# Down products of a two-chunk SwiGLU stage by seven block products, with one chunk's residual kept in DRAM

## The chip, the cores and the metric

One core of a Trainium2 chip runs the whole program. The metric is the device time of one execution in microseconds (us); the profile is one further execution, taken by the hardware profiler. TensorE appears as PE (its weight loads as PEld), VectorE as DVE, ScalarE as ACT, GpSimd as POOL and SyncE as SP. A transfer issued from SP and one issued from POOL go through different queues to the same 16 DMA engines.

## What is computed

A trunk of two layers over 1024 tokens of width 1024. Each layer has a token mixer and a SwiGLU network of inner width 2816, both behind an RMS norm with a learned shift and scale, both added to the residual x with a gate:

```python
for i in range(DEPTH):
    ...
    x = x + (1.0 + g_m)[:, None, :] * y
    h = modulate(rms_norm(x, norm_ffn_g[i]), sh_f, sc_f)
    y = swiglu_ffn(h, ffn_w_gate[i], ffn_w_up[i], ffn_w_down[i])
    x = x + (1.0 + g_f)[:, None, :] * y
return rms_norm(x, final_g)

def swiglu_ffn(h, w_gate, w_up, w_down):
    return (jax.nn.silu(h @ w_gate) * (h @ w_up)) @ w_down
```

The change concerns the last product, `@ w_down`, in a part of layer 1.

## The kernel before

**Layout.** Channels lie on the 128 partitions, tokens along a row. The tokens are cut into two chunks of 512, A and B. x is held as 8 tiles of 128x512 per chunk; the inner width is 22 tiles f of 128 channels.

**Precision.** A float32 operand is split into a rounded part (hi, a cast on ACT) and the rest (lo, a subtraction on DVE, or on early weights a negated copy on ACT and an accumulating transfer from POOL). A product of two such operands is three matmuls: hi by hi, hi by lo, lo by hi.

**The two-chunk part.** In layer 1 the tiles f = 8 to 21 are taken in 7 pairs for both chunks at once (`ffn_joint`). A pair has a gate unit and an up unit (`joint_unit`). In a unit the 2x2 block product (two halves of the width by two chunks, against two f tiles) is done with seven block products in place of eight, the scheme of Strassen and Winograd: blocks w11, w12, s2, s1, s3, s4 and w22, each of 4 steps of 3 matmuls, 84 in all. The sums s1 to s4 of the weights are made on DVE; the sums t1 to t4 of the activations are too large to be all in SBUF, so t1 and t4 lie in DRAM and are read into the same 8 buffers by turns in each unit (`streamed`, issued from SP).

**The down products** of a pair run inside the two units of the next pair, between those steps: after the steps counted in `GATE_SLOTS` and `UP_SLOTS` a unit calls `JointDowns.slot`, which makes one 128x512 output tile for one chunk: 2 f tiles by 3 matmuls into one of two spare PSUM banks, then `update` (a SCALAR_TENSOR_TENSOR on DVE: x = bank times gate plus x). Each unit has 8 such slots, 4 output tiles by two chunks; a pair has 16, or 96 matmuls. The downs of the last pair have no unit around them: `alone` runs them in two runs of 48 matmuls, between the first pieces of the chunk-B part that follows. The first pair of units instead carries the downs of chunk A for f = 6 and 7.

**Order.** The PE order is the order of the program text. The other engines are ordered by a scheduler with priorities; within an engine everything runs in that order, so an instruction that waits holds all behind it. Two PSUM pools matter here: `bank` (6 buffers, used in turn) and `spare_bank` (2 buffers).

**After the two-chunk part** chunk B does f = 0 to 7 alone (`ffn_mixed`), and `final(A)`, the last norm of chunk A, runs beside it.

Of the kernel before, what the change touches and what calls it, by code (L numbers as in the profile page):

```python
# [16 lines left out]
P = 128  # L17
# [55 lines left out]
for _name, _w in (  # L73
    ("ada_b", DEPTH * 6 * KT), ("norm_mix_g", DEPTH * KT), ("norm_ffn_g", DEPTH * KT),
    ("conv_b1", 2 * KT), ("conv_bdw", KT), ("conv_ln_g", KT), ("conv_ln_b", KT), ("conv_b2", KT),
    ("c", KT), ("pool_ls", KT), ("final_g", KT), ("conv_wdw", CW * KT),
):
    _COLS[_name] = _n
    _n += _w
NVEC = _n  # L80

# [41 lines left out]
def trunk(ctx, tc, xT, c, vec, ada, adan, w1, w2, wgu, wdn, wpl, wph, out):  # L123
# [43 lines left out]
    cst = ctx.enter_context(tc.tile_pool(name="cst", bufs=1))  # L167
    slots = ctx.enter_context(tc.tile_pool(name="slots", bufs=2 * KT))
# [132 lines left out]
    x = [[cst.tile([P, ch.n], F32, name=f"x_{ch.i}_{k}") for k in range(KT)] for ch in chunks]  # L301
# [9 lines left out]
    recip = cst.tile([P, PHALO], F32, name="recip")  # L311
# [4 lines left out]
    ccols = cst.tile([P, KT, 32], F32, name="ccols")  # L316
# [13 lines left out]
    uhalo = cst.tile([P, KT, HALO], F32, name="uhalo")  # L330
# [385 lines left out]
    class Taps:  # L716
# [10 lines left out]
        def step(self, e):  # L727
# [3 lines left out]
            w = lambda j: V("conv_wdw", j * KT + p)  # L731
# [47 lines left out]
    class Phased:  # L779
# [36 lines left out]
        def back(self):  # L816
            b = bank("pz")
            cols = b.rearrange("p (s q) -> p q s", q=PH)
            for q in range(PH):
                for g in range(PH):  # L820
                    matmul(cols[32 * g : 32 * g + 32, q, :], ident[:, 32 * q : 32 * q + 32], self.y[:, g * P : g * P + P], start=True, stop=True)
            clock["PE"] -= 2.5
            p = self.p
            u = st["u", 0, p]
            w = lambda j: V("conv_wdw", j * KT + p)
# [515 lines left out]
    def alone(downs, later=None):  # L1341

        def emit(take):
            if later is not None:
                later.fetch()
            while downs.todo:
                downs.slot(lambda n: output(n, True))
                if later is not None and len(downs.todo) == 4:
                    later.load(later.dps[0])
            reserve[0] = 0  # L1350
        return emit, ()
# [80 lines left out]
    class JointDowns(Downs):  # L1432


        def __init__(self, l, fs, dps, chs):
            super().__init__(None, l, fs, dps)
            self.todo = [(d, ch) for d in self.todo for ch in chs]

        def slot(self, out=None):
            d, ch = self.todo.pop(0)  # L1440
# [3 lines left out]
            for i, f in enumerate(self.fs):  # L1444
                g = st["g", ch.i, f]
                for j, (wp, a) in enumerate(((0, 0), (0, 1), (1, 0))):
                    matmul(b, wt[:, wp, i, (d % 2) * P : (d % 2 + 1) * P], g[a], start=i + j == 0, stop=i == 1 and j == 2)
            update(ch, d, b, gate_f, self.l)
            if d % 2 == 0:
                self.load(d // 2 + 1)  # L1450
            pace()
# [67 lines left out]
    def joint_unit(l, me, following, downs, later, first=False, last=False):  # L1519

        def emit(take):
# [8 lines left out]
            name = ("gate", "up")[me.which]  # L1530
            a, left, right = bank(name), bank(name), bank(name)
# [3 lines left out]
            slots_at = () if first else (GATE_SLOTS, UP_SLOTS)[me.which]  # L1535
            at = [0]

            def block(out, part, acts, start):
                for k, act in enumerate(acts):
# [5 lines left out]
                    if at[0] in slots_at and downs:  # L1545
                        for each in downs:
                            if each.todo:
                                each.slot()
                                break
            block(a, "w11", ha[:half], True)  # L1550
            S_.copy(ra, a)
            block(left, "w12", ha[half:], True)
            V_.tensor_tensor(ra, ra, left, op=ADD)
            if last:
# [5 lines left out]
            if first:  # L1560
                for each in downs:
                    while each.todo:
                        each.slot(lambda n: output(n, True))
                finish(T["rows"])
# [9 lines left out]
            else:  # L1574
                used[0] -= 2
# [3 lines left out]
            if later is not None:  # L1579
                later.load(later.dps[0])  # L1580
            block(right, "s4", hb[half:], False)
            V_.tensor_tensor(rb, rb, right, op=ADD)
            if last:
# [9 lines left out]
            if me.which == 0:  # L1593
# [3 lines left out]
            else:  # L1597
                sg = st["sg"]
                qa = temp(512)
                V_.tensor_tensor(ra, ra, sg[0], op=MUL)  # L1600
                V_.scalar_tensor_tensor(qa, a, -1.0, sg[3], op0=MUL, op1=MUL)
                V_.tensor_tensor(rb, rb, sg[1], op=MUL)
                V_.scalar_tensor_tensor(qb, qb, -1.0, sg[2], op0=MUL, op1=MUL)
                if len(st["G"]) == 2:
                    st["G"] += [raws.tile([P, D], F32R, tag="raw", name=nm("gpair")), wide("gpair", F32R)]
                for t, home, (ch, f) in zip((ra, qa, rb, qb), st["G"], ((A, 0), (A, 1), (B, 0), (B, 1))):
                    hi, lo = home[:, FRONT], home[:, BACK]
                    S_.copy(hi, t)
                    V_.tensor_tensor(lo, t, f32(hi), op=SUB)
                    st["g", ch.i, me.f + f] = hi, lo  # L1610
# [3 lines left out]
    def ffn_joint(l, start):  # L1614

        mates = [Joint(l, f, which) for f in range(start, NF, 2) for which in range(2)]
        mine = [[JointDowns(l, (start - 2, start - 1), dps, (A,)) for dps in ((0, 1), (2, 3))], []]
        for f in range(start, NF, 2):
            mine += [[JointDowns(l, (f, f + 1), dps, (A, B))] for dps in ((0, 1), (2, 3))]
# [110 lines left out]
    load_next(vecs, vec)  # L1730
    S_.activation(ccols[:, :, 0], V("c", 0, KT), AF.Silu)
    scale_b = cst.tile([P, KT], F32, name="scale_b")
# [311 lines left out]
    add(last[:1] + before[1:] + last[1:])  # L2044
# [56 lines left out]
```

## Time and profile before

| | before |
|---|---|
| median of 3 runs | 1777.24 us (1776.34 to 1777.5) |
| the profiled execution | 1779.4 us, of which its span is 1777.6 us |
| POOL busy in 1250 to 1550 us | 0 |
| DMA issues in 1250 to 1550 us | 162 of t (256 KB), 20 of gate and up weights and 10 of down weights (512 KB), all from SP |

The span is what the profile's page covers, from the first to the last instruction; the execution's own time is 1.8 us longer. A row of the timeline gives start, duration, engine, source line, operation, output<-input, and how many were merged. Rows of PE have modelled ends; the distance between starts is the better measure of what a matmul takes.

### The profile page before, as it was taken

What the parts mean: (1) busy time and instruction counts of PE and PEld (TensorE: products, weight loads), DVE (VectorE), ACT (ScalarE), POOL (GpSimd) and SP (SyncE); (2) the same over time, 40 slices, a digit from 0 to 9 for tenths busy, and PEclk for the clock granted to TensorE, in tenths of its full rate; (3) what the DMA queues carried; (4) which work ended last, traced back from release to release, by engine and by line L of the source; (5) the groups of instructions that cost most, each with busy time, mean ns of one, the idle gap of its engine ahead of it and who ended that gap; (6) DMA issues with size and microseconds to landing.
All of it is one profiled execution on the core that took longest, in us unless ns stands there. A gap on an engine that the chain in (4) does not pass through costs nothing.

```text
span 1777.6 us, 24497 instructions
## 1 busy us (share of the span) xinstructions
PE 1752.1 (99%) x8902; PEld 1471.4 (83%) x8902; DVE 1309.5 (74%) x2098; ACT 935.4 (53%) x1440; POOL 518.0 (29%) x551
## 2 busy tenths in 40 slices
PE   9999999999999999999999999999999999999997
PEld 7777687788888888899999888887888888888997
DVE  7999657887774228889996977886666566658885
ACT  4766656767756455555556356473333232334653
POOL 0599514988823112111103614310000000000012
PEclk9999999999999999999999999999999999999998
DMA  8958735989978988877765577796655555565651
GB/s 295 312 167 250 201 113 164 245 202 228 235 191 220 236 218 194 230 202 207 201 189 141 138 172 172 183 238 209 222 190 197 186 203 189 189 211 161 158 146 57
DMA packets 132652, 349.46 MB, mean 197 GB/s; under 512 B 13361, under 2 KB 24753, under 8 KB 132530
## 3 DMA queue, kind: packets, MB, share of 16 engines
q1 hardware_dynamic: 104656, 263.46, 43.6%
q0 software_dynamic: 26720, 83.37, 26.5%
q8 instruction: 70, 1.15, 0.3%
q10 hardware_dynamic: 1154, 1.05, 0.2%
q14 instruction: 52, 0.43, 0.1%
HBM read 338.40 MB, written 9.44 MB: 196 GB/s over the span
## 4 chain that ended last, share of the span: by engine, by line
PE 87%; DVE 4%; issue 3%; DMA 3%; POOL 1%; ACT 1%; SPq 0%; DVEq 0%; POOLq 0%; ACTq 0%
PE dn L140 24%; PE gate L140 23%; PE up L140 23%; PE y L140 6%; PE a L140 3%; PE g L140 3%; PE first L140 2%; DMA w<-in_wdn_dram 1%; DMA t<-t 1%; DVE x L117 1%; PE ada L140 1%; ACT w L117 1%; PE var L140 1%; PE rstd L140 1%; DMA adaw<-in_adan_dram 1%
## 5 line engine op out<-in xcount | busy, mean ns | idle before, releaser
L117 ACT CAST w<-raw 128x512 fp32r<-128x512 f32 (+1 forms) x338 | 277.0, 823 | 162.5 <-PE up L140 51.9
L117 DVE SCALAR_TENSOR_TENSOR x<-dn,gains,x 128x512 f32<-128x512 f32 (+1 forms) x360 | 261.2, 734 | 109.6 <-PE dn L140 108.0
L140 PE MATMUL dn<-ghi,w 128*128 128x512 f32 (+1 forms) x944 | 301.5, 384 | 2.0 <-DMA w<-in_wdn_dram 1.4
L140 PE MATMUL gate<-hhi,w 128*128 128x512 f32 (+1 forms) x968 | 293.8, 372 | 1.3 <-ACT hhi L117 0.8
L140 PE MATMUL up<-hhi,w 128*128 128x512 f32 (+1 forms) x968 | 294.5, 372 | 0.0
L117 ACT ACTIVATE w<-raw 128x1024 fp32r<-128x1024 f32 (+1 forms) x182 | 173.0, 950 | 187.1 <-PE up L140 58.0
L452 POOL DMA_DIRECT2D w<-in_wgu_dram x76 | 69.2, 910 | 632.5 <-ACT w L117 618.5
L140 PEld LDWEIGHTS gate<-hhi,w 128*128 128x128 f32 x968 | 177.8, 188 | 34.5 <-ACT hhi L117 1.0
L140 PEld LDWEIGHTS dn<-ghi,w 128*128 128x128 f32 x944 | 175.5, 188 | 35.9 <-DMA w<-in_wdn_dram 2.3
L140 PEld LDWEIGHTS up<-hhi,w 128*128 128x128 f32 x968 | 178.0, 188 | 31.8
L140 PE MATMUL dn<-gpair,w 128*128 128x512 f32 x744 | 188.4, 392 | 3.2 <-DMA w<-in_wdn_dram 3.1
L140 PE MATMUL dn<-glo,w 128*128 128x512 f32 (+1 forms) x472 | 181.2, 384 | 0.1
L140 PE MATMUL gate<-hlo,w 128*128 128x512 f32 (+1 forms) x484 | 180.0, 372 | 0.3 <-DVE hlo L117 0.3
L140 PE MATMUL up<-hlo,w 128*128 128x512 f32 (+1 forms) x484 | 179.8, 372 | 0.0
L117 DVE SCALAR_TENSOR_TENSOR ca<-u,vecs,ca 128x512 f32<-128x512 f32 x251 | 174.8, 746 | 0.9
L140 PEld LDWEIGHTS dn<-gpair,w 128*128 128x128 f32 x744 | 140.3, 189 | 34.1 <-DMA w<-in_wdn_dram 4.3
L117 DVE TENSOR_TENSOR w<-raw,w 128x512 fp32r<-128x512 f32 (+1 forms) x156 | 125.3, 808 | 32.1 <-ACT w L117 25.2
L117 POOL TENSOR_TENSOR pa<-pa,pr 128x512 f32<-128x512 f32 x92 | 131.7, 1513 | 8.4 <-ACT pr L117 6.4
L117 DVE TENSOR_TENSOR t<-t,up 128x512 f32<-128x512 f32 (+1 forms) x76 | 49.4, 650 | 99.1 <-PE up L140 96.5
L1206 POOL DMA_DIRECT2D w<-in_wgu_dram x42 | 37.2, 891 | 262.7 <-ACT w L117 115.9
L117 POOL TENSOR_TENSOR pa<-pa,ny 128x512 f32<-128x512 f32 x77 | 104.9, 1392 | 8.0 <-ACT ny L117 5.4
L140 PEld LDWEIGHTS gate<-hlo,w 128*128 128x128 f32 x484 | 91.1, 188 | 16.5 <-DVE hlo L117 0.6
(260 smaller groups left out, 3395.1 us busy)
## 6 DMA issues: line engine op xcount, KB each, us to landing
raw<-in_wgu_dram SPq DMA_DIRECT2D x148, 512.0 KB, 5.4
t<-t SPq DMA_DIRECT2D x224, 256.0 KB, 4.9
w<-in_wgu_dram POOLq DMA_DIRECT2D x76, 512.0 KB, 8.2
raw<-in_wdn_dram SPq DMA_DIRECT2D x74, 512.0 KB, 5.6
adaw<-in_ada_dram SPq DMA_DIRECT2D x64, 512.0 KB, 5.3
raw<-in_w_dram SPq DMA_DIRECT2D x42, 512.0 KB, 6.2
w<-in_wdn_dram POOLq DMA_DIRECT2D x34, 512.0 KB, 8.5
adaw<-in_adan_dram SPq DMA_DIRECT2D x32, 512.0 KB, 5.9
```

Source lines behind the costliest of these rows:

```text
L117: self.last = self.order(getattr(self.eng, name)(out, *args, **kw))
L140: last_mm[0] = nc.tensor.matmul(out, lhsT, rhs, start=start, stop=stop, **kw).ins.name
L452: order(nc.gpsimd.dma_start(as_src(lo), src, accum_op=ADD))
L1206: order(nc.gpsimd.dma_start(lo, src, accum_op=ADD))
```

## The change

The down products of the 7 pairs are done with seven block products as well. For each half of the output (`Seven`, two per pair) the four 128x256 pieces of the weights (two f tiles, a low and a high part of the output) are combined with the activations of two f tiles and two chunks. The seven blocks run in the order of `ORDER`, each for two output columns j: 14 slots per unit, with 3 matmuls each, after every second step of the unit (`SLOTS`).

- **Activations.** The up unit now makes seven pairs of hi and lo: g11, g21, g22 and the sums t1 to t4, in place of four (`given`).
- **Weights.** For each block a 128x256 hi and lo is made into a ring of four, three blocks ahead (`Ring.make`); s1 to s4 are sums on DVE.
- **Results.** Per column one bank serves w11, then s2, s3 and w22 on top of it (spare bank, "a"), another s1, s4, and then afresh w12 (ordinary bank, "e"). After s1, s2, s4 and s3 DVE adds the bank to chunk B's x. After w11, w12 and w22 ACT writes the bank, times the gate, into one of two 128x512 buffers (`st["scaled"]`, used in turn), and POOL issues an accumulating transfer of it to chunk A's x.
- **Chunk A's x** is written to DRAM in the first unit (`st["kept", "x"]`, 8 transfers on SP) and read back behind the last downs (`again`). Its SBUF buffers (pool `firsts`) hold t1 to t4 of the activations meanwhile.
- **Room.** Small constants are moved into three tiles (`spent`) which later hold weight pieces.

The diff, cut to its core:

```diff
-GATE_SLOTS = (6, 9, 12, 14, 17, 19, 22, 24)
-UP_SLOTS = (3, 6, 9, 11, 14, 17, 20, 23)
+SLOTS = range(2, 29, 2)
+ORDER = ("w11", "s1", "s2", "s4", "s3", "w12", "w22")
+MADE_AHEAD = 3
...
+    class Ring:
+        def make(self, count):
+            if self.tiles is None:
+                whole = [wts.tile([P, D], F32R, tag="w", name=nm("ring")) for _ in range(2)]
+                self.tiles = [t[:, o : o + QUAD] for t in whole for o in (0, QUAD)]
+            for _ in range(count):
...
+                with tc.high_priority(offset=-PREPARED):
+                    src = downs.source(block)
+                    S_.copy(hi, src)
+                    V_.tensor_tensor(lo, src, f32(hi), op=SUB)
...
+    class Seven:
+        def fetch(self):
...
+            for (f, h), t in self.raw.items():
+                nc.sync.dma_start(t, wdn[self.l, self.fs[f], :, h * QUAD + first : h * QUAD + first + H])
...
+        def slot(self, out=None):
+            block, j = self.todo.pop(0)
+            on = "a" if block in ("w11", "s2", "s3", "w22") else "e"
+            if block == "w11":
+                self.banks["a", j] = spare_bank("dn")
+            if block == "s1":
+                self.banks["e", j] = bank("dn")
+            b = self.banks[on, j]
+            wt = ring.made[self, block]
+            act = st["blocks"][{"w11": "g11", "s1": "t1", "s2": "t2", "s4": "g22", "s3": "t3", "w12": "g21", "w22": "t4"}[block]]
+            for i, (wp, a_) in enumerate(((0, 0), (0, 1), (1, 0))):
+                matmul(b, wt[wp][:, j * P : (j + 1) * P], act[a_], ...)
...
+            if block in ("w11", "w12", "w22"):
+                at, scale = (high, minus) if block == "w22" else (low, plus)
+                t = st["scaled"][st["turn"] % 2]
+                st["turn"] += 1
+                S_.activation(t, b, AF.Copy, scale=scale)
+                order(nc.gpsimd.dma_start(st["kept", "x"][at], t, accum_op=ADD))
+            else:
+                at, scale = (low, plus) if block in ("s2", "s4") else (high, minus)
+                V_.scalar_tensor_tensor(x[1][at], b, scale, x[1][at], op0=MUL, op1=ADD)
+            if j == 1:
+                ring.make(1)
+            pace()
...
+            def given(key, t):
+                hi, lo = st["blocks"][key]
+                S_.copy(hi, t)
+                V_.tensor_tensor(lo, t, f32(hi), op=SUB)
...
+                st["kept", "x"] = [kept.tile([P, 512], F32, name=nm("x")) for _ in range(KT)]
+                for dst, t in zip(st["kept", "x"], x[0]):
+                    sync.dma_start(dst, t)
...
+            if up:
+                V_.tensor_tensor(rb, rb, sg[1], op=MUL)
+                V_.tensor_tensor(sg[1], qb, rb, op=SUB)
+                given("t3", sg[1])
+                V_.tensor_tensor(rb, ra, rb, op=SUB)
+                given("t1", rb)
+                V_.scalar_tensor_tensor(qb, rb, -1.0, qb, op0=MUL, op1=SUB)
+                given("t2", qb)
...
-            mine += [[JointDowns(l, (f, f + 1), dps, (A, B))] for dps in ((0, 1), (2, 3))]
+            mine += [[Seven(l, (f, f + 1), half)] for half in range(2)]
...
+    def again(take):
+        x[0] = x_first()
+        for t, src in zip(x[0], st["kept", "x"]):
+            sync.dma_start(t, src)
+    add(last[:1] + before[1:] + last[1:] + [(again, ())])
```

**What stands on PE now.** In the first block of an up unit of the two-chunk part, before; `up` is the unit's own product, `dn` the downs of the pair before, with its activations (`gpair`) and its weight (`w`):

```order
L140 MATMUL up_13030<-hlo_9812,w_12900 128x512
L140 MATMUL up_13030<-hhi_9811,w_12900 128x512
L140 MATMUL dn_13047<-gpair_11130,w_12962 128x512 x3
L140 MATMUL dn_13047<-gpair_11340,w_12962 128x512 x3
L140 MATMUL up_13030<-hhi_9813,w_12900 128x512
L140 MATMUL up_13030<-hlo_9814,w_12900 128x512
```

The end of that block now: the downs take 3 matmuls of one block (`ring` is the block's weight), after every second step:

```order
L142 MATMUL up_12656<-hlo_9817,w_12524 128x512
L142 MATMUL up_12656<-hhi_9816,w_12524 128x512
L142 MATMUL dn_12685<-gpair_11133,ring_11797 128x512 x3
L142 MATMUL up_12657<-hhi_9818,w_12527 128x512
L142 MATMUL up_12657<-hlo_9819,w_12527 128x512
```

Each visit to the downs is half as long, and there are 14 in a unit in place of 8.

**What stands on ACT now.** Around the end of an up unit, before: casts of the next units' weights (`w`) and of the pair's activations (`gpair`), and the copy of the next unit's first bank:

```order
L117 CAST gpair_11130<-t_13033 128x512
L117 CAST gpair_11806<-t_13035 128x512
L117 CAST w_13175<-raw_12931 128x512
L117 CAST w_13211<-raw_13036 128x512
L117 CAST gpair_11805<-t_13034 128x512
L117 CAST w_13311<-raw_13036 128x512
L117 CAST gpair_11340<-t_13263 128x512
L117 COPY t_13279<-gate_13276 128x512
L117 CAST w_13387<-raw_13178 128x512
L117 CAST w_13390<-raw_13178 128x512
```

The same place now; `scaled` are the two buffers, written from a bank `dn` (of w12's second column first, then w22's two), and every one of these three waits for the transfer that last read its buffer (DMASW counts transfers issued from POOL, DMAHW those from SP):

```order
L119 ACTIVATE scaled_11795<-dn_12180,gains 128x512 [waits DMASW3_49,PE_49]
L119 ACTIVATE scaled_11795<-dn_12141,minus 128x512 [waits DMASW4_49,PE_49,Activation_49]
L119 CAST t_2272_11669<-sg_12117 128x512 [waits DVE_49]
L119 CAST w_12280<-raw_12023 128x512 [waits DMAHW2_49,PE_49]
L119 CAST ring_11797<-acc_12335 128x256 [waits PE_49]
L119 CAST t_2268_11665<-t_12128 128x512 [waits DVE_49]
L119 CAST gpair_11343<-t_12391 128x512 [waits DVE_49]
L119 ACTIVATE scaled_11795<-dn_12153,minus 128x512 [waits DMASW5_49,PE_49,Activation_49]
L119 CAST t_2270_11667<-t_12129 128x512 [waits DVE_49]
L119 COPY t_12401<-gate_12398 128x512 [waits PE_49]
L119 CAST w_12524<-raw_12283 128x512 [waits DMAHW3_49]
```

Between the two writes for w22 stand five casts, and the copy of the next unit's first bank (`t` from `gate`) stands behind both.

**What stands on POOL now.** Before, from the end of the first unit to the part after, POOL's queue held two transfers in a row which lie 374 us apart on the timeline:

```order
L1241 DMA w_11359<-in_wdn_dram 128x2x256
L1241 DMA w_11365<-in_wdn_dram 128x2x256
L1241 DMA w_11369<-in_wdn_dram 128x2x256
L1206 DMA w_11393<-in_wgu_dram 128x512
L452 DMA w_14490<-in_wgu_dram 128x1024
L452 DMA w_14497<-in_wgu_dram 128x1024
L452 DMA w_14631<-in_wgu_dram 128x1024
```

Now the accumulating transfers to chunk A's x lie between them, 84 in all; the first ones:

```order
L1215 DMA w_11396<-in_wgu_dram 128x512 [waits DMASW6_49,PE_49,Activation_49]
L1535 DMA x_11500<-scaled_11795 128x512 [waits DMAHW0_49,DMASW4_49,Activation_49]
L1535 DMA x_11501<-scaled_11795 128x512 [waits DMAHW2_49,DMASW5_49,Activation_49]
L1535 DMA x_11500<-scaled_11795 128x512 [waits DMASW4_49,Activation_49]
L1535 DMA x_11501<-scaled_11795 128x512 [waits DMASW7_49,DMASW5_49,Activation_49]
L1535 DMA x_11504<-scaled_11795 128x512 [waits DMAHW5_49,DMASW0_49,Activation_49]
L1535 DMA x_11505<-scaled_11795 128x512 [waits DMAHW6_49,DMASW1_49,Activation_49]
L1535 DMA x_11502<-scaled_11795 128x512 [waits DMAHW3_49,DMASW2_49,Activation_49]
```

A transfer to the same tile of x (w11's and w12's) waits for the earlier one; the two halves of the output use different tiles.

More of the change, by code (lines that the diff above doesn't have):

```diff
@@ L80 @@
 NVEC = _n
+NTAPS = CW * KT
 class Chunk:
@@ L1347, in emit @@
                 downs.slot(lambda n: output(n, True))
-                if later is not None and len(downs.todo) == 4:
+                if later is not None and len(downs.todo) == 4 and not isinstance(later, Seven):
                     later.load(later.dps[0])
-            reserve[0] = 0
+            reserve[0] = 2 if isinstance(later, Seven) else 0
         return emit, ()
@@ L1534, in emit @@
                 later.fetch()
-            slots_at = () if first else (GATE_SLOTS, UP_SLOTS)[me.which]
+            slots_at = () if first else SLOTS
             at = [0]
@@ L1549, in block @@
                                 break
+            def given(key, t):
[3 more added lines that the diff above has]
+            if up:
+                sg = st["sg"]
+                if "blocks" not in st:
+                    g11, g21 = st["G"]
+                    g22 = raws.tile([P, D], F32R, tag="raw", name=nm("gpair"))
+                    st["blocks"] = {key: (g[:, FRONT], g[:, BACK]) for key, g in (("g11", g11), ("g21", g21), ("g22", g22))}
+                    for key in ("t1", "t2", "t3", "t4"):
+                        st["blocks"][key] = [firsts.tile([P, 512], F32R, tag="x", name=nm(key)) for _ in range(2)]
             block(a, "w11", ha[:half], True)
@@ L1578, in emit @@
             V_.tensor_tensor(qb, qb, a, op=ADD)
-            if later is not None:
-                later.load(later.dps[0])
+            if up:
+                V_.scalar_tensor_tensor(qb, qb, -1.0, sg[2], op0=MUL, op1=MUL)
+                given("g22", qb)
+            if later is not None and ring.tiles is None:
+                minus = st["minus"] = tmp.tile([P, KT], F32, tag="minus", name="minus", bufs=1)
+                V_.tensor_scalar(minus, gate_f[:, l * KT : (l + 1) * KT], -1.0, None, op0=MUL)
+                s_ = wide("scaled")
+                st["scaled"], st["turn"] = (s_[:, :512], s_[:, 512:]), 0
+                st["pieces"] = [spent[n] for n in ("taps", "halos", "ccols")] + [tmp.tile([P, Q], F32, tag="rows", name=nm("piece"), bufs=1)]
+                ring.make(MADE_AHEAD)
             block(right, "s4", hb[half:], False)
             V_.tensor_tensor(rb, rb, right, op=ADD)
+            if up:
+                V_.tensor_tensor(rb, rb, sg[1], op=MUL)
[5 more added lines that the diff above has]
+                given("t2", qb)
             if last:
@@ L1592, in emit @@
                 st["t1"] = streamed("t1", B)
-            if me.which == 0:
+            if not up:
                 st["sg"] = [window(512, "sg") for _ in range(3)] + [temp(512, "ny", 2)]
@@ L1597, in emit @@
             else:
-                sg = st["sg"]
                 qa = temp(512)
-                V_.tensor_tensor(ra, ra, sg[0], op=MUL)
                 V_.scalar_tensor_tensor(qa, a, -1.0, sg[3], op0=MUL, op1=MUL)
[L1602 to L1610, printed above, removed]
+                given("g21", qa)
+                V_.scalar_tensor_tensor(qa, qb, -1.0, qa, op0=MUL, op1=SUB)
+                given("t4", qa)
             pace()
```

80 lines of the change are left out of this document (63 added, 17 removed).

## The prediction

> **What bounds the kernel now.** I read the page's first part for the busiest engine, then its chain, then the stage.
>
> ```profile
> PE 1752.1 (99%) x8902; PEld 1471.4 (83%) x8902; DVE 1309.5 (74%) x2098; ACT 935.4 (53%) x1440; POOL 518.0 (29%) x551
> PE 87%; DVE 4%; issue 3%; DMA 3%; POOL 1%; ACT 1%; SPq 0%; DVEq 0%; POOLq 0%; ACTq 0%
> ```
>
> TensorE sets the end. In the part that the change touches it is without a gap; these are the windows of one pair (a gate and an up unit) and of 50 us of the same stage (length, then busy time and count of PE, PEld, DVE, ACT and POOL, granted clock, DMA share, GB/s):
>
> ```profile
> 1250.43:1310.27 59.84, 59.84 (x266) 49.57 (x264) 35.21 (x53) 18.35 (x32) 0.00 (x0) 1.00 0.54 185
> 1300.00:1350.00 50.00, 50.00 (x223) 41.40 (x222) 31.80 (x50) 15.62 (x27) 0.00 (x0) 1.00 0.59 206
> ```
>
> The clock is full, DVE is idle for 40% of the pair, ACT for 70%, POOL always. So fewer matmuls are worth their full time, as long as nothing new makes PE wait.
>
> What one matmul takes is read from two starts on the timeline; the third row is the DVE reading the finished bank:
>
> ```profile
> 1254.51 1.52 PE L140 MATMUL dn<-gpair,w 128*128 128x512 f32 x6
> 1255.87 0.39 PE L140 MATMUL gate<-hhi,w 128*128 128x512 f32 x1
> 1256.07 0.75 DVE L117 SCALAR_TENSOR_TENSOR x<-dn,gains,x 128x512 f32<-128x512 f32 x1 [0.89 <-PE dn L140]
> ```
>
> Six take 1.36 us, so one takes 0.2267 us; a bank is read 0.2 us after the next product starts. A pair now has 2 x 84 products of its own and 96 downs: 264 x 0.2267 = 59.85 us, the 59.84 of the window.
>
> **1. Products removed: -19.0 us.** A pair's downs become 2 halves x 7 blocks x 2 columns x 3 = 84 matmuls. Over 7 pairs 84 fewer, x 0.2267 = 19.0 us. A unit around a `Seven` is 14 x (6 + 3) x 0.2267 = 28.6 us, 2.04 per slot, where it was 29.9.
>
> **2. The two buffers of `scaled`.** This is what is new on the path. A write by ACT must wait until the transfer before last has landed, and six writes follow one another: w12's two, w22's two at the end of a unit, w11's two at the start of the next. Counted from a unit's start, the slots end at 22.4 and 24.5 (w12), 26.5 and 28.6 (w22). w22's banks are the two spare ones, which the next unit's w11 needs again at 29.9 and 32.0 (its slots start 1.36 after the 28.6, then 2.04 later). What a round through a buffer costs, from rows of before: how long such a write takes, when POOL issues after ACT began, and how long the 42 accumulating transfers of 256 KB of one line took to land (median, then its ends):
>
> ```profile
> 1261.56 0.59 ACT L117 COPY t<-gate 128x512 f32<-128x512 f32 x1 [2.78 <-PE gate L140]
> 1641.74 0.63 ACT L117 ACTIVATE w<-raw 128x512 fp32r<-128x512 f32 x1
> 1642.78 0.87 POOL L1206 DMA_DIRECT2D w<-in_wgu_dram  x1 [7.85 <-ACT w L117]
> w<-in_wgu_dram POOLq DMA_DIRECT2D x42, 256.0 KB, 5.5
> DMA to landing us min/median/max: 3.6/5.5/10.6
> ```
>
> The write is 0.6 us, the issue comes 1.04 us after the write starts, and the landing, counted from the issue, is L. w12's second write starts at 24.5 + 0.2, is issued at 25.7, lands at 25.7 + L; then w22's second write takes 0.6 and PE, due at 32.0, may go on. The wait is 25.7 + L + 0.6 - 32.0 = **L - 5.7 us**, near enough L - 5.6 with a tenth for the handover (an estimate), at each of the 12 unit ends behind a `Seven`. The first columns have the same slack, and their transfer starts 2 us sooner. w11's writes in the next unit are due at its fifth slot, 38.1 and 40.1: with L below 7 they are in time. The five casts that the order puts between w22's two writes take some 3 us of ACT (starts 0.5 apart) and are hidden behind that wait.
>
> So L decides. The transfers of before write SBUF from DRAM; one that adds to DRAM isn't in the trace, and nothing excludes that it is quicker or slower. Single ones, with the window of the 5 us behind each issue:
>
> ```profile
> w<-in_wdn_dram POOLq DMA_DIRECT2D x1, 256.0 KB, 4.2
> 1208.92:1213.92 5.00, 4.74 (x15) 3.30 (x15) 1.80 (x3) 0.62 (x1) 2.14 (x2) 0.66 0.63 95
> w<-in_wdn_dram POOLq DMA_DIRECT2D x1, 256.0 KB, 6.8
> 1192.49:1197.49 5.00, 5.00 (x24) 4.14 (x23) 5.00 (x10) 3.98 (x8) 1.22 (x1) 1.00 1.06 323
> w<-in_wdn_dram POOLq DMA_DIRECT2D x1, 256.0 KB, 9.0
> 1199.63:1204.63 5.00, 5.00 (x24) 4.14 (x23) 5.00 (x9) 2.29 (x4) 1.19 (x1) 1.00 0.84 205
> ```
>
> 4.2 us with the DMA engines at 0.63, 6.8 with them full, 9.0 once. And at a unit's end they are full: this is the read-back of t1, 8 transfers issued by SP some 2 us before the next unit's first product, and the windows behind it.
>
> ```profile
> 1278.27 4.49 SPq L150 DMA_DIRECT2D t<-t  x8
> 1280.35 0.39 PE L140 MATMUL up<-hhi,w 128*128 128x512 f32 x1
> 1280.00:1286.00 6.00, 6.00 (x28) 4.97 (x27) 3.34 (x6) 2.21 (x4) 0.00 (x0) 1.00 0.95 349
> 1286.00:1293.00 7.00, 7.00 (x32) 5.82 (x31) 4.00 (x6) 0.62 (x1) 0.00 (x0) 1.00 0.32 108
> ```
>
> w12's second transfer is issued half a microsecond into this burst. The row that it is nearest to is the 6.8; since the burst has only begun, I take L = 6.3. The wait is 0.7 us, 12 times: **+8.4 us**. The ends: nothing at the 3.6 of the shortest, 3.4 x 12 = 41 us at 9.0.
>
> The Trainium skill, page "DMA: Bandwidth & Descriptors", section "Queues, rings and completion order", has each DMA engine serve the queues that have work in turn, packet by packet. By that rule POOL's transfers and SP's burst slow each other, and the 4.2 against the 6.8 agrees with it.
>
> **3. Work on DVE, ACT and SP that PE covers: 0.** The order has 81 DVE instructions per pair, 22 of them 256 wide, for 53 (all 512 wide) in the window. Those 53 took 35.2 us, 0.66 each; a 256-wide one is bounded by
>
> ```profile
> L117 DVE TENSOR_TENSOR tf<-hf 128x256 f32<-128x256 f32 x8 | 3.3, 415 | 0.0
> ```
>
> That makes 59 x 0.66 + 22 x 0.42 = 48 us of the new pair's 57.1, and 33 x 0.66 + 11 x 0.42 = 26 us of the 28.6 in an up unit, the fuller one. ACT gains 12 writes, 3 casts and a net 6 half-wide ones: under 12 us on top of 18.4. Weights are made three blocks, 12 us, ahead. All this fits, so it costs nothing; an up unit with little room left is the weak place (a rival).
>
> **4. The start: +1.** Chunk A's x is stored by SP in the first unit, ahead of the first read-back of t4, which was only just in time before:
>
> ```profile
> 1219.77 6.34 SPq L150 DMA_DIRECT2D t<-t  x9
> 1229.48 1.16 PE L140 MATMUL gate<-t,w 128*128 128x512 f32 x3 [0.17 <-DMA t<-t]
> ```
>
> SP's queue moved 263.46 MB in 43.6% of the span, so at 340 GB/s:
>
> ```profile
> q1 hardware_dynamic: 104656, 263.46, 43.6%
> q0 software_dynamic: 26720, 83.37, 26.5%
> ```
>
> 8 x 256 KB are 6.2 us of transfer. Most falls where the engines were at 0.63 (1208.92 to 1213.92); between 0 and 6.2 I take 1.
>
> **5. The end: +3.5.** In `alone` the slots follow each other every 0.68 us, without a unit's own products. w12's first write is ready at 7.7, its transfer lands 1.04 + 5 later, near 13.7, and only then can w22's first write start, though PE is done at 9.5. Behind the first run PE has 48 products (10.9 us) before it needs ACT. Behind the last it has 24 narrow ones:
>
> ```profile
> 1643.35 10.88 PE dn L140 x48
> 1654.23 10.01 PE gate L140 x84
> ```
>
> 84 in 10.01 us, so 24 last 2.9: PE arrives at 12.4 and needs a copy that ACT does behind w22's write, at some 14.9. That is 2.5 us (0 with L = 3.6, 6 with 9.0). The read-back of x stands in SP's queue ahead of later weights and waits for the last transfers: 0 to 4, I take 1.
>
> **Sum.** -19.0 + 8.4 + 1 + 3.5 = -6.1. Against the profiled execution's 1779.4 that is 1773.3; the median of the runs lies 2.2 lower, so **1771 us**.
>
> **Rivals.**
> - *The transfers are not in the way* (L at 5.5 or less, the median). For: 5.5 is the middle of 42. Against: the burst. Terms 2 to 5 shrink to 0 + 1 + 1.5: about 1761.
> - The Trainium skill, same page, section "Anatomy of one DMA — SWDGE (gpsimd) path", gives 2.0 us plus the bytes over 436 GB/s: an estimate of 2.6 us for 256 KB, by which that rival would hold. The trace disagrees; no such transfer took less than 3.6.
> - *The transfers become the bound* (slower). POOL's queue moves 83.37 MB in 26.5% of the span, 177 GB/s, half of SP's rate: 1.5 us of all engines per 256 KB, 12 per pair, 18 us on top of 0.54 x 59.84 = 32 of a pair: 50 of 57. Then the loaded landing is the rule, and the next unit's w11 writes are late too. It decides at L = 6.8, where the 12 waits (14.4) and the ends eat the 19.0; at 9.0 the sum is -19 + 41 + 1 + 4.5 = +27, about 1804.
> - *DVE becomes the bound in up units*, held up by casts that stand behind a waiting ACT write. At 2 us over in 7 up units, 14 us on the forecast: 1785.
> - That the saving isn't made is excluded: the order has 42 matmuls in each of the 14 `Seven`.
>
> **How the numbers follow.** The measurement can tell about 0.2% (3.6 us) from no change. The forecast's case (L from 5.6 to 7) has 0.50: 0.30 faster, 0.17 the same, 0.03 slower. Transfers out of the way 0.17, all faster. Transfers as the bound 0.20, slower. DVE 0.13: 0.04 the same, 0.09 slower. In all faster 0.47, same 0.21, slower 0.32. The range: from 1761, the second case, to 1795, which is L = 8; about 0.2 is left beyond.
>
> **What would show it.** Right: in the stage 84 downs per pair, PE with a gap of 0.5 to 1.5 us at each unit's end, put down to ACT writing `scaled`, which waits for the DMA to x; those landing in 6 to 7 us. Wrong: landings near 4 or 9; gaps inside a unit behind DVE (`ring`, t1 to t4); gaps of several us at the start or behind the last downs. An accumulating write to DRAM that behaves unlike those into SBUF would upset it most.

## The result, and the profile after

| | before | after |
|---|---|---|
| median of 4 runs each | 1776.79 us (1776.11 to 1777.5) | 1805.24 us (1803.47 to 1807.13) |
| ratio | 1 | **1.016**, 95% interval 1.0143 to 1.0178 |
| the profiled execution, its span | 1779.4, 1777.6 us | 1803.47, 1801.7 us |

The changed kernel is slower by 1.6%; 1771 us was predicted. The spans of the two profiled executions differ by 24.1 us, the medians by 28.5: the profiled execution of after is its fastest, that of before lies above its four timed runs, and the 4 us between the two figures can't be placed. One of the ten executions of kernel 12 below was in a slow state (4049.57 us) and is left out of its ratio.

The page of after, its busy shares, its chain and the landing of the new transfers:

```profile
PE 1744.0 (97%) x8818; PEld 1457.3 (81%) x8818; DVE 1370.7 (76%) x2274; ACT 1011.6 (56%) x1615; POOL 590.9 (33%) x635
PE 70%; issue 14%; DMA 8%; DVE 5%; POOL 3%; ACT 1%; POOLq 0%; DVEq 0%; SPq 0%; ACTq 0%
x<-scaled POOLq DMA_DIRECT2D x84, 256.0 KB, 5.8
```

TensorE issues the 84 matmuls less (8902 to 8818) and is busy 8 us less, but the span is 24 us longer: PE now waits. Its share of the chain fell from 87% to 70%; DMA, 3% before, stands for 8%, and "issue", time in which the engine waited for nothing that the profile shows, rose from 3% to 14%. Where the 24.1 us arise is read from the starts of PE's first products of the units on the timeline:

| stretch, us | before | after | |
|---|---|---|---|
| start to the first two-chunk gate | 1194.27 | 1197.79 | +3.5 |
| the first two units (no `Seven`) | 56.16 | 55.12 | -1.0 |
| the 12 units with a `Seven` | 360.10 | 361.69 | +1.6 |
| the tail: from there to the end | 167.07 | 187.10 | +20.0 |

So three things ask for a reason: a stage that should have become 16 us shorter and did not, a tail that lost 20, and 3.5 us far ahead of any changed product.

**The stage.** The windows of after that answer to those of before (length, busy time and count of PE, PEld, DVE, ACT and POOL, clock, DMA share, GB/s), and one round through a buffer of `scaled`, from ACT's, POOL's and PE's timelines:

```profile
1252.91:1614.60 361.69, 348.37 (x1514) 283.77 (x1512) 266.89 (x480) 178.38 (x344) 63.30 (x73) 1.00 0.91 247
1300.00:1350.00 50.00, 45.88 (x195) 37.16 (x193) 36.58 (x66) 22.89 (x46) 7.79 (x9) 0.97 0.86 248
1308.15 0.68 ACT L119 ACTIVATE scaled<-dn,gains 128x512 f32<-128x512 f32 x1
1309.24 0.88 POOL L1535 DMA_DIRECT2D x<-scaled  x1 [1.33 <-ACT scaled L119]
1317.09 0.69 ACT L119 ACTIVATE scaled<-dn,minus 128x512 f32<-128x512 f32 x1 [3.02 <-DMA x<-scaled]
1317.83 1.55 PE L142 MATMUL dn<-gpair,ring 128*128 128x512 f32 x3 [2.39 <-ACT scaled L119]
```

This is the chain that the prediction drew: w12's second write at 1308.15, its issue 1.09 us later, its landing 7.8 us after the issue, only then, at 1317.09, w22's second write into the same buffer, and PE's w11 products 2.39 us late. The view of the tile `scaled` over the stage sums it up, who waited for ACT's writes and how long the transfers took:

```profile
  PE dn L142: 13.1, 11
DMA to landing us min/median/max: 3.8/5.8/9.0
```

The median mixes two kinds. Of the 14 transfers of each place in a `Seven`, those of w11's two copies and of w12's first landed in 4.1 to 4.2 us (median), those of w12's second and of w22's two in 6.3 to 7.2. The eleven that PE's waits hang on (w12's second) took 5.7 to 7.8 us, 6.55 in the mean.

**The tail.** Its 20.0 us are 9.6 in the first run of downs that stands alone, 3.1 in the second, 6.9 in the 84 narrow products behind that, and 0.4 in all the rest. The first run: the window of its 42 matmuls, and the waits in it, of PE and of ACT:

```profile
1625.48:1645.91 20.43, 12.72 (x43) 8.36 (x42) 19.72 (x40) 11.81 (x24) 5.29 (x6) 0.92 0.60 121
1631.85 3.05 PE L142 MATMUL dn<-t,ring 128*128 128x512 f32 x6 [3.49 <-ACT scaled L119]
1629.04 0.62 ACT L119 CAST w<-raw 128x512 fp32r<-128x512 f32 x1 [1.70 <-DMA raw<-in_wgu_dram]
1638.88 0.97 PE L142 MATMUL dn<-t,ring 128*128 128x512 f32 x3 [1.23 <-DVE x L119]
1641.24 0.93 PE L142 MATMUL dn<-gpair,ring 128*128 128x512 f32 x3 [1.39 <-DVE x L119]
1643.73 0.97 PE L142 MATMUL dn<-gpair,ring 128*128 128x512 f32 x3 [1.57 <-DVE x L119]
```

42 matmuls need 9.5 us and take 20.4. The four waits of PE are 7.7 us of the difference; in the 4 us behind the first of them the granted clock was 0.57. DVE is busy for 19.7 of the 20.4 us (third pair of the window): the updates of x stand among the sums and low parts that prepare chunk B's next units, and each bank must be read before the next block may be added to it. ACT's copy of w11's bank stands behind a cast that waits for a weight's load. Behind the second run PE waits once more, for an ordinary copy that stands on ACT behind w22's write, and then works for 4 us at a clock of 0.50:

```profile
1677.29 0.69 ACT L119 ACTIVATE scaled<-dn,minus 128x512 f32<-128x512 f32 x1 [5.70 <-DMA x<-scaled]
1678.29 0.58 PE L142 MATMUL gate<-thi,shi 128*128 128x256 f32 x1 [4.49 <-ACT t L119]
```

**Ahead of the stage.** SP's queue of after has two loads of weight pieces at 308 and 318 us that the program has some 900 us later: their buffers are free from early on, so the scheduler moved them up, into a stretch where the DMA engines are full. PE's wait there, before (first row) and after (last row):

```profile
321.59 0.73 PE L140 MATMUL dn<-ghi,w 128*128 128x512 f32 x2 [1.21 <-DMA w<-in_wdn_dram]
308.29 0.36 SPq L1501 DMA_DIRECT2D ccols<-in_wdn_dram  x1
317.89 0.33 SPq L1501 DMA_DIRECT2D piece<-in_wdn_dram  x1
322.46 1.22 PE L142 MATMUL dn<-ghi,w 128*128 128x512 f32 x2 [2.79 <-DMA w<-in_wdn_dram]
```

### The profile page after: what moved, and what is told of

The parts are those of the page before. It is cut to its first block, busy times and chain, and to the rows that moved or that the text cites. A ratio compares the mean times of both kernels' runs of the same rounds, so it can differ in the third digit from the quotient of the medians.

```text
span 1801.7 us, 25051 instructions
## 1 busy us (share of the span) xinstructions
PE 1744.0 (97%) x8818; PEld 1457.3 (81%) x8818; DVE 1370.7 (76%) x2274; ACT 1011.6 (56%) x1615; POOL 590.9 (33%) x635
## 3 DMA queue, kind: packets, MB, share of 16 engines
q0 software_dynamic: 38816, 105.40, 34.3%
## 4 chain that ended last, share of the span: by engine, by line
PE 70%; issue 14%; DMA 8%; DVE 5%; POOL 3%; ACT 1%; POOLq 0%; DVEq 0%; SPq 0%; ACTq 0%
PE gate L142 18%; PE dn L142 17%; PE up L142 16%; PE y L142 6%; DMA x<-scaled 4%; PE a L142 4%; PE g L142 3%; PE first L142 2%; POOL x L1535 2%; DVE x L119 1%; DMA w<-in_wdn_dram 1%; DMA t<-t 1%; DVE t L119 1%; PE ada L142 1%; DMA w<-in_wgu_dram 1%
## 5 line engine op out<-in xcount | busy, mean ns | idle before, releaser
L119 ACT CAST w<-raw 128x1024 fp32r<-128x1024 f32 (+1 forms) x310 | 260.5, 842 | 97.8 <-PE up L142 39.2
L119 DVE SCALAR_TENSOR_TENSOR x<-dn,gains,x 128x512 f32<-128x512 f32 (+1 forms) x304 | 219.2, 731 | 52.5 <-PE dn L142 51.1
L1535 POOL DMA_DIRECT2D x<-scaled x84 | 73.4, 874 | 359.4 <-ACT scaled L119 297.8
L119 DVE SCALAR_TENSOR_TENSOR ca<-u,taps,ca 128x512 f32<-128x512 f32 x251 | 174.9, 746 | 0.9
L119 DVE TENSOR_TENSOR w<-raw,w 128x512 fp32r<-128x512 f32 (+1 forms) x128 | 106.1, 835 | 57.8 <-ACT w L119 33.5
L1215 POOL DMA_DIRECT2D w<-in_wgu_dram x42 | 37.2, 892 | 238.2 <-ACT w L119 84.1
L142 PEld LDWEIGHTS up<-hlo,w 128*128 128x128 f32 x484 | 91.2, 188 | 15.9
```

The lines of the kernel that those rows point to most:

```text
L119: self.last = self.order(getattr(self.eng, name)(out, *args, **kw))
L142: last_mm[0] = nc.tensor.matmul(out, lhsT, rhs, start=start, stop=stop, **kw).ins.name
L1215: order(nc.gpsimd.dma_start(lo, src, accum_op=ADD))
L1535: order(nc.gpsimd.dma_start(st["kept", "x"][at], t, accum_op=ADD))
```

## The experiments

Theory A: PE waits for the landing of transfers, with two buffers. A2: the transfers' traffic delays other loads. B: the order of work on ACT and DVE. C: the loads moved up are the loss ahead of the stage. D: the runs that stand alone lose what DVE and ACT can't do in time there. All numbers by stretch are from the starts of PE's products, as above; "12 units" are those with a `Seven` in after. Kernels 1 to 7 and 9 were timed once each, 8 four times, 10 ten, 11 five and 12 ten times, on four chips; on these the kernel before had medians of 1773.5 to 1777.0 us, and its single runs lay between 1773.5 and 1780.1. A total of a single run is therefore good to some 3 us; the stretches are the better measure.

| kernel | us | first gate | 12 units | of them the last | tail |
|---|---|---|---|---|---|
| before | 1776.79 | 1194.3 | 360.1 | 31.0 | 167.1 |
| after | 1805.24 | 1197.8 | 361.7 | 30.5 | 187.1 |
| 1 transfers read g22 | 1795.32 | 1197.1 | 352.5 | 29.3 | 187.8 |
| 2 no transfers | 1780.62 | 1198.6 | 342.7 | 28.6 | 180.6 |
| 3 all piece loads tied | 1807.71 | 1194.1 | 364.5 | 30.9 | 193.2 |
| 4 only the first half-1 loads tied | 1801.70 | 1195.8 | 362.1 | 31.5 | 187.3 |
| 5 preparing task later | 1809.14 | 1199.6 | 363.0 | 32.7 | 188.5 |
| 6 blocks in spread order | 1818.57 | 1198.3 | 381.6 | 42.9 | 181.4 |
| 7 last pair by the old scheme | 1789.24 | 1196.8 | 369.3 | 34.3 | 166.8 |
| 8 the edits of 4, 6 and 7 | 1798.50 | 1197.3 | 375.9 | 37.2 | 167.7 |
| 9 spread order, t1 sooner | 1787.35 | 1196.6 | 353.4 | 38.1 | 180.9 |
| 10 all edits | 1773.01 | 1194.5 | 353.7 | 37.9 | 168.4 |
| 11 all edits, less DMA at the end | **1763.43** | 1193.4 | 345.9 | 30.1 | 166.3 |
| 12 before, with that last edit alone | 1776.96 | 1194.7 | 359.9 | 30.8 | 166.5 |

### 1 and 2: what the transfers cost

```diff
-                order(nc.gpsimd.dma_start(st["kept", "x"][at], t, accum_op=ADD))
+                order(nc.gpsimd.dma_start(st["kept", "x"][at], f32(st["blocks"]["g22"][0]), accum_op=ADD))
```

> Each accumulating transfer to chunk A's x keeps its size, its destination and its place in POOL's queue, but reads a half of g22 (an operand of the down products, which is not rewritten while a transfer reads it) in place of the tile that ACT has just written; so chunk A's rows are given other summands, and ACT's scaled copies wait for no landing any more. Theory A (ACT waits for the landing of the last transfer but one, and with it PE): the 12 units that hold a Seven fall from 361.7 us to 343 to 348, the waits of PE on the scaled copy at unit starts (13 us) vanish, and of the tail's 187 us some 7 to 12 go; in all 1778 to 1786. Theory A2 (the transfers' traffic itself holds up other loads): no change, 1800 or more. Theory B (the order of work on ACT and DVE, whatever the transfers do): 355 to 361 in the 12 units, 1797 to 1804.

The second leaves the transfers out.

> Leaves out the 84 accumulating transfers: chunk A's x lacks the down sums of g11, g21 and t4's products; ACT still writes its scaled copies, without a wait. Theory A: as the kernel whose transfers read g22, within 3 us, 1778 to 1786. Theory A2: 10 us or more shorter than that kernel, under 1790 while that one is over 1800. Theory B: 1797 to 1804.

Without transfers the 12 units take 342.7 us, and PE has no gap in them at all, though ACT and DVE do all their new work:

```profile
1255.50:1598.20 342.70, 342.70 (x1514) 283.76 (x1513) 266.36 (x479) 177.23 (x341) 1.74 (x2) 1.00 0.62 208
```

So the saving is made, 17.4 us against 360.1, and the transfers cost 19.0 of it; theory B falls for these units. Without the wait but with the traffic (kernel 1) only 9.2 of the 19.0 come back, less than theory A expected, and the two kernels are 14.7 us apart where it allowed 3. PE has no wait for `scaled` left in the units, but in five of the six gate units one for the read-back of t4, as here:

```profile
1456.03 0.50 PE L142 MATMUL gate<-t,w 128*128 128x512 f32 x1 [0.87 <-DMA t<-t]
1457.13 0.72 PE L142 MATMUL gate<-t,w 128*128 128x512 f32 x2 [0.60 <-DMA t<-t]
```

That wait is kernel 1's own: after has none for a read-back in these units. As every transfer waits for g22 in place of ACT's writes, POOL issues the 12 of a pair in some 25 us (1305.93 to 1331.24 on its timeline) and then none for 33 us, where after spreads them over the pair. So kernel 1 shows that bunched transfers delay read-backs, and not how much of the 19.0 in after is of that kind. In the tail kernel 1 lost what it should have won. The wait behind the second run is gone (10.0 us for 84 narrow products, as before), but in the first run ACT's cast waited 4.69 us for its weight, and PE behind it:

```profile
1624.29 0.62 ACT L119 CAST w<-raw 128x512 fp32r<-128x512 f32 x1 [4.69 <-DMA raw<-in_wgu_dram]
1627.11 1.22 PE L142 MATMUL dn<-t,ring 128*128 128x512 f32 x2 [7.67 <-ACT scaled L119]
```

With no transfers at all the tail is still 13.5 us longer than before's, 12.0 of them in the first run: that part is not theirs.

### 3 and 4: the loads that were moved up

```diff
+                d = nc.sync.dma_start(t, wdn[...])
+                tc.add_manual_dep(d.ins, last_mm[0], edge, reason="behind the products")
```

> The 56 loads of the seven-block scheme's raw weights (128x256 each) are tied behind the last product that stands ahead of them in the program, so none of them can move to 300 us into the program. Theory C (the loads of pieces that were moved up there delay the fetches of that stage): PE reaches the first two-chunk gate 3 to 5 us earlier than the 1197.8 of the changed kernel, the 281 to 331 us stretch is again as before the change, total 1799 to 1802. Rival: the stretch is longer for another reason (the order of other loads changed too), the first gate stays at 1197 to 1198 and the total within 2 us of 1803.5.

> Of the raw weights' loads only those of the first half-1 Seven, the four whose buffers are free from early on, are tied behind the last product ahead of them in the program. Theory C: PE reaches the first two-chunk gate at 1194 to 1195 us of the span as with all loads tied (1194.1; 1197.8 with none), the stage and the tail stay within 2 us of the changed kernel's 361.7 and 187.1; total 1799 to 1801. Rival: the early loads had nothing to do with it, 1803 or more.

The first gate is reached at 1194.1 and 1195.8. PE's wait at that place, here in kernel 4, stands between its two values in before and after:

```profile
321.78 0.98 PE L142 MATMUL dn<-ghi,w 128*128 128x512 f32 x2 [1.88 <-DMA w<-in_wdn_dram]
```

Single profiles scatter by some 2 us here, so all kernels count: the five with these loads tied (3, 4, 8, 10, 11) reach the first gate at 1193.4 to 1197.3, mean 1195.0, the seven of the changed form with untied ones at 1196.6 to 1199.6, mean 1197.8. The place itself separates them without overlap: PE's wait there is 2.53 to 2.85 us in the seven with untied loads, and 1.16 to 2.00 in the five tied ones and the two of the old scheme (before and kernel 12). Theory C holds, at 2.8 us in the mean; kernels 4 and 8, tied, still lost 2.3 us at this place against before. As a whole kernel 3 is slower, with 2.8 us more in the 12 units and 6.1 more in the tail; which of its later loads causes that was not traced.

### 5: the preparing task later

```diff
-    put_eager(("T", 1), lambda: combined(B, (A, A, B, B)))
-    add(last[:1] + before[1:] + last[1:] + [(again, ())])
+    add(last[:1])
+    put_eager(("T", 1), lambda: combined(B, (A, A, B, B)))
+    add(before[1:] + last[1:] + [(again, ())])
```

> The task that prepares chunk B's rows for the paired units behind the two-chunk part is started behind the first run of downs that stand alone in place of ahead of it. Theory D (DVE is full in that run: this task's 8 sums, 8 halves and 8 low parts stand between the updates and the ring's blocks): the run of 42 downs that takes 20 to 26 us from the last up unit's end shortens by 5 to 9 us, total 1795 to 1800. Rival (PE waits there for the scaled copies' landing alone): no more than 2 us shorter, and the task is late for its own units later on: 1803 to 1808.

Inconclusive: the scheduler put the task's sums on DVE where they were, ahead of the updates, and the tail is 188.5. The program's order did not decide here.

### 6 and 9: the writes spread over the unit

```diff
-ORDER = ("w11", "s1", "s2", "s4", "s3", "w12", "w22")
+ORDER = ("s1", "w11", "s4", "s2", "w12", "s3", "w22")
...
+            if block == "s4":
+                V_.tensor_tensor(t, s, a11, op=ADD)
```

> The blocks of each Seven run in the order s1, w11, s4, s2, w12, s3, w22 (s4's weights cost one 128x256 sum more); so the pairs of scaled copies stand 3, 2 and 2 blocks apart (8 to 12 us between a copy into a buffer and the next into the same one) where they stood 1, 1 and 5 apart (4 us). Number of buffers, transfers and products unchanged. Theory A (a buffer is asked for before its transfer has landed): the 15 us that PE waits for the scaled copy at unit starts fall to 0 to 3, the 12 units take 345 to 353 us of 361.7; total 1786 to 1796. Theory A2 (traffic: the transfers delay the read-back of t4 and t1): the 5 to 10 us that the transfers from g22 left in the stage stay, 350 to 354. Theory B (any order shows the same waits): 358 us or more, total over 1800.

PE's waits for `scaled` are gone in the stage, and a larger one has come: s1, now first, needs t1, which the up unit ahead hands over only near its end, behind t3. Gate units take 32.8 us, up units 28.6:

```profile
1316.74 0.50 PE L142 MATMUL dn<-t,ring 128*128 128x512 f32 x1 [1.11 <-ACT t L119]
1318.39 1.22 PE L142 MATMUL dn<-t,ring 128*128 128x512 f32 x2 [1.14 <-DVE t L119]
1316.70:1320.70 4.00, 2.81 (x7) 2.02 (x8) 2.84 (x5) 1.24 (x2) 0.22 (x1) 0.66 1.08 319
```

The number missed its range by 28 us, yet the wait that it was about had left. (In the last unit, 42.9 us, DVE waited 12.77 us for the load of a weight piece, and PE 9.18 behind it.) So the wait for t1 was taken away too, on top of the new order:

```diff
-SLOTS = range(2, 29, 2)
+SLOTS = (6, 7, 9, 11, 12, 14, 16, 18, 20, 21, 23, 25, 27, 28), range(2, 29, 2)
...
-            slots_at = () if first else SLOTS
+            slots_at = () if first else SLOTS[me.which]
...
-                given("t3", sg[1])
                 V_.tensor_tensor(rb, ra, rb, op=SUB)
                 given("t1", rb)
+                given("t3", sg[1])
```

> The spread order again, with its own new wait taken away: in the gate units the first block (s1, which needs t1) stands at slot 6 in place of 2, the other blocks closer together, and in the up units t1 is handed over ahead of t3. Theory A and its sequel (the landing waits are gone in the spread order; the 2.3 us that PE waited for t1 in each gate unit, with the clock drop behind, is all that is left of it): gate units 28.6 to 30 us in place of 32.8, the 11 units up to the last one 314 to 325 us. Rival (the slots that stand closer together now wait for their banks, or the read-backs are late): gate units 31 us or more. The last unit and the tail stay as in the spread order, about 40 and 181 us; total 1790 to 1803.

```profile
1251.32:1566.57 315.25, 315.00 (x1388) 259.66 (x1386) 257.99 (x460) 164.78 (x316) 55.52 (x65) 1.00 0.95 254
```

The 11 units ahead of the last take 315.3 us (331.2 in after, 314.2 with no transfers), with the same transfers, the same two buffers and the DMA engines at 0.95. The transfers land no sooner (median 5.6 us against 5.8), but ACT waits for them 12 times, 14.0 us in all, where it waited 36 times, 70.8 us, and PE never. What has changed is the order of the blocks and their slots, t1 ahead of t3, and one half-wide sum more: the same landings cost nothing where the writes stand apart. With kernel 2 this shows theory A for the stage. The last unit kept a wait like kernel 6's:

```profile
1596.08 0.43 DVE L119 TENSOR_TENSOR acc<-halos,piece 128x256 f32<-128x256 f32 x1 [9.24 <-DMA piece<-in_wdn_dram]
```

### 7: the last pair by the old scheme

`Seven` is replaced by `JointDowns` for the last pair, chunk B first, and the last up unit hands over g12 in place of t1 to t4; the core of the edit:

```diff
-            mine += [[Seven(l, (f, f + 1), half)] for half in range(2)]
+            if f + 2 < NF:
+                mine += [[Seven(l, (f, f + 1), half)] for half in range(2)]
+            else:
+                mine += [[JointDowns(l, (f, f + 1), dps, (B, A))] for dps in ((0, 1), (2, 3))]
```

> Only the last pair (f = 20 and 21) takes its down products by the old scheme, 6 matmuls for each of 16 downs, chunk B's before chunk A's, in the two runs that stand alone; chunk A's x is loaded back at the last unit's end. 12 more products of 6 us in sum than the changed kernel has there. Theory D (in the runs that stand alone each product waits for a bank that DVE or ACT has yet to read, or for a block that they have yet to make, as nothing else stands between): the tail from the last unit's end takes 167 to 172 us in place of 187, total 1784 to 1790. Rival (the tail is late because of the transfers still under way and the reload): 178 us or more, total over 1794.

The tail takes 166.8 us, with 12 matmuls more (2.7 us at 0.2267 each; the expectation has 6): all 20 us are back. The last run again, with DVE full and PE none the less without a gap:

```profile
1648.00:1664.30 16.30, 16.30 (x74) 13.49 (x73) 16.30 (x28) 7.56 (x14) 1.72 (x2) 1.00 0.58 150
```

A product of the old scheme has a bank of its own and one update at its end; in a `Seven` each block waits for the reading of the one ahead. The 12 units lost 7.6 us, 3.8 of them in the last, in which that pair's weights and x are now loaded too. PE's waits for `scaled` in them are 19.3 us in 12 places, against 13.1 in 11; why those landings came later was not traced.

### 8, 10, 11 and 12: together

> The three edits together: blocks in the spread order, the last pair by the old scheme, the first half-1 loads tied. If the three causes are separate, their gains add up: -3.5 upstream, -8 to -16 in the 12 units, -15 to -20 in the tail, 1764 to 1777, a ratio of 0.993 to 1.000 to the kernel before. If they share one cause (DMA queues that are full), less than two thirds of the single gains' sum: 1780 or more.

Kernel 8 took 1798.50 us, which is where the expectation put causes that are shared. But its three edits had cost or won, one by one, -3.5 (4), +13.3 (6) and -16.0 (7): from 1805.24 that is 1799.0, so they do add up. Kernel 6's wait for t1 was not foreseen. Kernel 10 has the edits of 9, 7 and 4, and the reload of x on POOL's queue:

```diff
-                        sync.dma_start(t, src)
+                        order(nc.gpsimd.dma_start(t, src))
```

> That order, the last pair by the old scheme, the first half-1 loads tied, and chunk A's x loaded back by POOL's queue, behind the transfers into it, in place of SP's, ahead of the next weights. If the causes found add up: first gate at 1195 to 1197, 11 units 314 to 325, the last unit 29 to 33 (37 with the reload on SP's queue), tail 167; total 1764 to 1776, ratio 0.993 to 1.000. If the last unit's loads are late for another reason than the reload, it stays at 35 to 38 and the total at 1772 to 1782.

1773.01 us, ratio 0.9982 (0.997 to 0.9994). The 11 units (315.8), the tail and the first gate came within 1.5 us of what was expected; the last unit did not, with PE waiting four times for t4, 5.1 us:

```profile
1564.80:1602.68 37.88, 32.52 (x127) 24.61 (x126) 19.35 (x31) 17.54 (x29) 10.91 (x14) 0.88 1.01 277
1592.93 0.73 PE L142 MATMUL up<-t,w 128*128 128x512 f32 x2 [2.03 <-DMA t<-t]
1600.39 1.22 PE L142 MATMUL up<-t,w 128*128 128x512 f32 x2 [1.83 <-DMA t<-t]
```

So moving the reload did not help; the engines were full (1.01). Kernel 11 takes traffic out there:

```diff
+    before = [own(u) for u in before]
```

> As the kernel with all edits together, and besides the low parts of the weights of the plain gate and up that follow the last unit are made by DVE (raw less high part) in place of accumulating transfers on POOL's queue: three or four fetches of 512 KB less on the DMA engines, in the stretch in which they were at 1.0 or more and PE waited 7 us for t4 to be read back. If full DMA engines make the last unit late: it falls from 37.9 us to 29 to 32, the rest unchanged, total 1764 to 1768, ratio to the kernel before 0.993 to 0.996. Rival (the read-backs are issued too late whatever the traffic is, or DVE's 1.3 us subtractions take the place of the wait): 35 us or more, total 1770 or more.

> The kernel before with that last edit alone (low parts by DVE in place of accumulating transfers, for the plain gate and up behind the last unit). Its last unit has no wait for t4, so nothing is to be gained there: within 0.1% of the kernel before, if the gain of the combined kernel comes from room on the DMA engines. Rival (the edit is worth as much without the change): 3 us or more faster than before.

```profile
1563.62:1593.73 30.11, 28.86 (x128) 23.57 (x126) 21.65 (x33) 15.30 (x27) 5.77 (x7) 1.00 0.96 282
```

The last unit falls to 30.1 us, and PE has no wait for t4 left. The read-backs of t4, issued 13 to 18 us into the unit in both kernels, land in 4.6 to 8.3 us where they took 7.0 to 17.5 in kernel 10: the loads were not issued later, they took longer. The total is **1763.43**, ratio **0.9928** (0.9916 to 0.9941) to the kernel before, 12.1 us less than before's median on the same chip; the same edit alone on before gives 1.0 (0.999 to 1.0009). Of the difference of the profiled spans, 17.6 us, 14.2 lie in the 12 units; the 1.7 in the first two units are scatter, for kernel 12, which has the old scheme, has them too (53.8 us there against 56.2 in before).

## Why the prediction was wrong, step by step

- **Step 1, products removed (-19.0): right.** 17.4 us in the 12 units without transfers (16.3 worked out; the other 2.7 belong to the tail), and units of 28.56 us, as predicted.
- **Step 2, the two buffers (+8.4): the mechanism right, the size not.** It measured +19.0 (361.7 against 342.7). The place, the chain and nearly the landing came as drawn: L was 6.55 where 6.3 was taken. 13.1 us are PE's waits at 11 unit starts, 1.19 each, so the slack in the formula was 5.4 where 5.6 was worked out. The other 5.9 the formula didn't have: the units are longer by some 0.3 us beyond each wait, and by 1.9 in the one behind whose wait the clock fell to 0.57. Of the 10.6 us that the step missed, 5.9 are thus what a wait costs beyond itself, and 4.7 small errors of L and of the slack, taken 11 times.
- **Step 3, work on DVE, ACT and SP that PE covers (0): right in the units, wrong outside.** Kernel 2 shows no PE gap in 342.7 us. The rival of a DVE bound in up units fell; but the step looked at the stage only, and the same work has no cover in the runs that stand alone.
- **Step 4, the start (+1): no cost seen.** 55.1 us in the first two units, between the 56.2 and 53.8 of the two kernels with the old scheme (before and 12).
- **Step 5, the end (+3.5): this is the step that failed most.** It let the slots of `alone` follow each other every 0.68 us and counted ACT's writes alone. With step 1's share of -2.7 the tail should have changed by +0.8; it changed by +20.0. 13.5 are there without any transfer: blocks that wait for a bank to be read, by a DVE that is full and by an ACT in order behind casts, one of which waits for a weight. In kernel 2 PE's waits there are 4.1 us for ACT and 3.6 for DVE, and in the 16 us behind the first its clock stood at 0.50 and then 0.64. 6.5 come with the transfers, above all the 4.49 us behind the second run, which the step had at 2.5 with a landing of 5 us, where w12's took 7.8. That these runs are at fault is shown by kernel 7 (it moves the reload of x as well, but 12.0 of the 13.5 arise in the first run, ahead of any reload); how the 13.5 divide between DVE, ACT and the clock was read from the trace, not tried apart (kernel 5 did not move the work).
- **Not in the prediction: loads that the scheduler moves up, +3.5.** 2.8 by the two groups of kernels. The prediction had no term for it; the order of SP's queue would have told of it.

-17.4 + 19.0 - 1.0 + 20.0 + 3.5 = +24.1, the difference of the spans. The rival that came true in sign is the one of the transfers as the bound, but not by its mechanism: the landing that counts stayed below its point of decision, L = 6.8, w11's transfers landed in 4.1 to 4.2 us (median), so that the loaded landing was not the rule, and it set the ends at +1 + 4.5 (where step 5 has 6 for the same L) and needed L = 9 for a loss of this size. The rival of L at 5.5 or less fell with the 6.55.

## To carry to other kernels

A scheme that saves products by chaining blocks through one bank needs other products between the blocks; where they stand alone, use the plain scheme. Look at how evenly writes through a small ring of buffers are spaced before asking for more buffers: here a new order of the seven blocks, with one operand handed over sooner, let two buffers suffice. And a load whose buffer is free early may be issued early: tie it, or read its queue's order.

## What the runs showed of the hardware

After some waits PE's granted clock fell to half, for 3.4 or 6.8 us (behind the wait of 2.39 us from 1317.96 to 1321.38, behind that of 2.79 from 321.27 to 328.10), and it does not follow the wait's length alone. The windows of 4 us of after that begin where the wait ended: 1.55 us waited, 2.39, 2.79 (the row at 322.46), 2.31 and 4.49:

```profile
1286.60:1290.60 4.00, 4.00 (x18) 3.31 (x19) 0.84 (x2) 1.91 (x4) 0.94 (x2) 1.00 1.10 310
1317.80:1321.80 4.00, 3.97 (x10) 3.12 (x11) 2.32 (x4) 2.99 (x6) 1.65 (x2) 0.57 1.08 351
322.40:326.40 4.00, 3.94 (x9) 3.14 (x10) 1.29 (x2) 2.17 (x3) 4.00 (x5) 0.50 1.06 275
1659.90:1663.90 4.00, 3.96 (x17) 3.30 (x18) 2.86 (x6) 2.43 (x5) 1.62 (x2) 1.00 1.02 147
1678.30:1682.30 4.00, 4.00 (x19) 4.00 (x20) 0.61 (x1) 3.49 (x7) 2.60 (x3) 0.50 0.90 176
```

About 10 matmuls are issued in 4 us at 0.5 to 0.57, against 18 (the last row has products of half the width, 19 against some 33): such a wait costs some 2 us more than its length. Even the same wait in the same program text differs: at 203 to 205 us all fourteen kernels have one of 2.98 us, and the 4 us behind it had a clock of 1.00 in five of them and of 0.50 to 0.67 in nine. So a profile's stretches scatter by the clock alone. The Trainium skill, page "TensorE: Matmul & The Clock Gate", section "HAM oscillation — how this bites in real kernels", warns of idle gaps above about 3.4 us; here gaps of 2.39 and 2.79 us sufficed, and one of 2.31 did not; in kernel 4 the gap of 1.88 us sufficed (0.57).

An accumulating transfer of 256 KB into DRAM landed in 5.8 us (median; 3.8 to 9.0), close to those into SBUF of before (5.5; 3.6 to 10.6): adding to DRAM was not what upset the forecast.
